# A decoder layer with routed experts on one core: the turn from the router to the first expert rearranged

## Chip, cores, metric
One of the eight cores of one Trainium2 chip runs the whole kernel. Times are device microseconds (us) of one execution; less is better. MiB below is 1,048,576 bytes.

## What is computed
Input: 256 tokens of width 2048 in float32, one condition vector `c`, and the weights of one layer. Cut to what matters here:

```python
mod = silu(c) @ w_ada + b_ada                  # six vectors: sh1, sc1, gt1, sh2, sc2, gt2
h = rmsnorm(x, g1) * (1 + sc1) + sh1
mixed = concat(recurrence(h @ w_in), attention(h @ w_in)) @ w_out
x = x + gt1 * mixed
h = rmsnorm(x, g2) * (1 + sc2) + sh2
group = argmax of 4 group logits; two best of its 8 experts; weights = softmax(two) * p_group
y = sum over the 2 chosen experts e of weight_e * (silu(h @ w_gate[e]) * (h @ w_up[e])) @ w_down[e]
out = rmsnorm(x + gt2 * y, g_final)
```

There are 32 experts of 12 MiB each, and all of them are run, each on at most 64 tokens (slots); a branch at the end covers an overflow.

## The kernel before
The order of the work is written out by hand: each engine runs its instructions strictly in program order, and a tile's first reader waits for its writer. All weights come through one queue, SP's. `load` appends to a list, and `pump` (line 122) issues the head of the list as soon as a 1 MiB slot is free, so loads go in list order and a load waits behind every earlier one. There are 7 slots `w` from the start; 3 `x` and 2 `TT` are added during the output projection and 3 `v` at its end, 15 in all. `drop` gives a slot back after its last reader.

**Projection stage.** The work runs in units of half a MiB of weight. `split(i + 3)` prepares the pieces of a unit three units ahead: ACT rounds the weight to `wh` (line 453), DVE makes the rest `wl` (line 456). PE then runs 24 short or 12 long matmuls on it (lines 462 to 470). First come 20 tiles of `w_in`. Between them go 12 pairs of tiles of `w_ada` for sc1 and sh1 (`pair_load`, after the tiles whose numbers stand in `PAIRS`); each pair is used by an event (`gem`), half of it on PE (line 358) and half on DVE (line 352), and after four pairs `fold1` (line 388) makes a quarter of h from them. Then come 28 more tiles of `w_in` with 64 rows of `w_ada` (1 MiB each, for sc2, sh2, gt1, gt2 in this order) spread between them by `ROWS_B`; a row costs four matmuls (`row`, `product`) or two DVE instructions. Attention and recurrence run beside as jobs, some steps after each unit.

**Output projection.** Two halves (`part` 1, then 0) of four column blocks `n` of four units each. `out_evac` ends a block: in part 0 DVE adds the two halves (957), multiplies by gt1 (958) and adds x into `xp` (960), each for the two halves `m` of the tokens, and ACT squares for the norm (962). Two units later `router_part` transposes `xp` into `h2t` on PE (975), copied out by ACT (979) and DVE (977), and one unit after that `router_logits` (988) adds to the 36 logits. For the last block these stand alone at the end.

**Turn.** `rs2` is the norm's factor (POOL's power, 110). Lines 1125 to 1178 choose: the logits `el`, the first maximum of the group logits, then of the experts, that one masked out, and the first maximum again, with the weights in between; the choice `sel` goes through three matmuls (1173 to 1175) to slot numbers. `one_hots` makes the matrices G and Sg, `gather` (1210) collects the tokens of two experts into XT in four quarters `kq`, `back` prepares the way back.

**Experts.** They run in pairs. `gate_up` takes four pieces per expert, each of one gate and one up tile, and drops both tiles after the piece. Between pieces stand, for the first pair, the spread of gt2 (`gate`, lines 776 and 777), the overflow count and `natural` (the residual copied to `xr` by ACT). Then come the next pair's gather and `down` (eight tiles).

Of the kernel before, what the change touches and what calls it, by code (L numbers as in the profile page):

```python
# [16 lines left out]
P = 128  # L17
# [23 lines left out]
PAIRS = (0, 2, 3, 5, 7, 8, 10, 12, 13, 15, 17, 18)  # L41
AHEAD = 8
ROWS_B = (3, 2, 3, 2, 2, 2, 2) * 4
# [12 lines left out]
def layer_kernel(ctx: ExitStack, tc: tile.TileContext, x, c, w_ada, b_ada, g_norm_mix, w_in, lb_logits,  # L56
# [158 lines left out]
    assert not rows  # L215
# [732 lines left out]

    def out_evac(part, n):
        sl = slice(512 * n, 512 * n + 512)  # L950
        xin = None if part else take(("x", n // 2))[:, :, 512 * (n % 2):512 * (n % 2) + 512]
        for m in range(2):
            if part:
                ACT.activation(tok[8 + n][:, m, :], banks["o"][m], AF.Copy)
                continue
            tmp = right["ex1"].tile([P, 512], F32, name="tmp", tag="tmp", bufs=TB)
            DVE.tensor_tensor(tmp, banks["o"][m], tok[8 + n][:, m, :], op=ALU.add)
            DVE.tensor_tensor(tmp, tmp, vec[GT1][:, sl], op=ALU.mult)
            xs = right["xp"][:, m, 4 * n:4 * n + 4, :]
            DVE.tensor_tensor(xs.rearrange("t r p -> t p r"), xin[:, m].rearrange("t (p r) -> t p r", r=4),  # L960
                              tmp.rearrange("t (p r) -> t p r", r=4), op=ALU.add)
            ACT.activation(tmp, xs.rearrange("t r p -> t (r p)"), AF.Square, accum_out=right["ss4"][:, m, n:n + 1])
        if not part and n % 2:
            free.append((mixa, f"TT{n // 2}"))
            drop(("x", n // 2))

    def router_part(n):

        xp, ht = right["xp"], right["ex1"].tile([P, 4, S], F32, name="h2t", tag="h2t", bufs=1)
        for b in range(2):  # L970
            t = mx()
            tv = t.rearrange("p (a s) -> p a s", a=2)
            for a in range(2):
                for m in range(2):
                    PE.transpose(tv[:, a, m * P:m * P + P], xp[:, m, 4 * n + 2 * b + a, :], ident)
            if b:
                DVE.tensor_copy(ht[:, 2:4, :], tv)
            else:
                ACT.activation(ht[:, 0:2, :], tv, AF.Copy)
        return ht  # L980

    def router_logits(n, ht):
        if not n:
            banks["r"] = hold("lg")[0]
        for r in range(4):
            k = 4 * n + r
            for m in range(2):
# [38 lines left out]
    for i, u in enumerate(units):  # L1026
# [31 lines left out]
        else:  # L1058
            first, last = u["kq"] % 2 == 0 and not u["half"], u["kq"] % 2 and u["half"]
            bk, k0 = "o", (4 * u["kq"] + 2 * u["half"] + 8) % 16  # L1060
            if not u["part"] and not u["n"] and first:
# [3 lines left out]
                open_router()  # L1065
        if first:
# [3 lines left out]
        for r in range(2):  # L1070
# [38 lines left out]

    ht = router_part(3)  # L1110
# [14 lines left out]
    for m in range(2):  # L1125
        DVE.scalar_tensor_tensor(el[:, m], banks["r"][:, 64 * m:64 * m + 36], rs2[:, m:m + 1], cb, op0=ALU.mult, op1=ALU.add)

# [6 lines left out]
    def first_max(vals, n, wts):  # L1134

        v, q, w = rt(), rt(n), rt()
        DVE.tensor_reduce(v, vals, axis=AX.X, op=ALU.max)
        DVE.tensor_tensor(q, vals, bcast(v[:, :, None], [P, 2, n]), op=ALU.is_equal)
        DVE.tensor_tensor(q, q, bcast(wts[:, None, :], [P, 2, n]), op=ALU.mult)
        DVE.tensor_reduce(w, q, axis=AX.X, op=ALU.max)  # L1140
        DVE.tensor_tensor(q, q, bcast(w[:, :, None], [P, 2, n]), op=ALU.is_equal)
        return v, q

    gl, ee = el[:, :, 0:4], el[:, :, 4:36]
    gmx, gsel = first_max(gl, 4, w4)
    gex, pg = rt(4), rt()
    DVE.tensor_tensor(gex, gl, bcast(gmx[:, :, None], [P, 2, 4]), op=ALU.subtract)
    ACT.activation(gex, gex, AF.Exp)
    DVE.tensor_reduce(pg, gex, axis=AX.X, op=ALU.add)
    DVE.reciprocal(pg, pg)  # L1150
    em = rt(NE)
    emv = em.rearrange("p m (g e) -> p m g e", g=4)
# [366 lines left out]
```

## Time and profile before
| | us |
|---|---|
| median of 3 runs | 1568.62 (1567.92 to 1569.22) |
| profiled execution, its own time | 1570.29 |
| its span, first to last instruction | 1568.5 |
| PE busy | 1495.2 (95%) |
| DVE busy | 641.4 (41%) |
| ACT busy | 378.1 (24%) |

The profiled execution lies 1.67 us above the median of the runs. The mean granted clock of TensorE was 0.977 of its full 2.4 GHz; the lower level is 1.2 GHz, shown as 0.50. In a timeline row the first two numbers are the start and the length of a merged group in us, then come the engine, the line, the operation, output<-input and the count, and in brackets how long the engine stood idle before and who released it. PE's busy share is modelled and also covers waits inside a stream of matmuls, so it doesn't say alone that PE is the bound.

### The profile page before, as it was taken

The numbers are of one execution on the slowest core, as the hardware profiler recorded it, in microseconds if no ns is written. First come the engines' busy times: TensorE is split into PE (matmuls) and PEld (weight loads), VectorE is DVE, ScalarE is ACT, GpSimd is POOL, SyncE is SP. The second block draws the span as 40 slices with busy tenths as digits, with TensorE's granted clock in tenths as the row PEclk, the third lists the DMA queues.
The fourth block names the chain that finished last, engine by engine and source line by source line (L and its number), as shares of the span: only waits on it lengthen the run. The fifth ranks groups of instructions, "written<-read, shape, count | busy, mean of one in ns | idle before, by whom it ended". The sixth has DMA issues, their size and how long they took to land. (4 is left out here: it accounts for less than half of the span.)

```text
span 1568.5 us, 21452 instructions
## 1 busy us (share of the span) xinstructions
PE 1495.2 (95%) x8911; PEld 873.5 (56%) x8911; DVE 641.4 (41%) x1193; ACT 378.1 (24%) x666; POOL 12.5 (1%) x23
## 2 busy tenths in 40 slices
PE   5799989999999987999999999999999999999996
PEld 2687877877678765434443553553554544544532
DVE  3566887556465553132332322332322322232224
ACT  3344332452535523211110110110110101101112
POOL 0000000000000000000000000000000000000000
PEclk9889999999999997999999999999999999999998
DMA  9989989979994654999999999999999999999995
GB/s 355 310 293 333 330 343 396 378 308 350 361 380 155 221 184 195 423 420 421 421 421 421 421 421 421 421 421 421 421 421 421 421 421 421 420 421 421 421 410 205
DMA packets 128271, 579.15 MB, mean 369 GB/s; under 512 B 16983, under 2 KB 17063, under 8 KB 71847
## 3 DMA queue, kind: packets, MB, share of 16 engines
q1 hardware_dynamic: 128170, 577.74, 92.2%
q8 instruction: 72, 1.18, 0.3%
q14 instruction: 29, 0.24, 0.0%
HBM read 575.60 MB, written 2.10 MB: 368 GB/s over the span
## 5 line engine op out<-in xcount | busy, mean ns | idle before, releaser
L1300 DVE TENSOR_TENSOR xr<-st,xr 128x512 f32<-128x512 f32 x124 | 84.4, 690 | 364.6 <-PE st L1299 364.6
L1239 PE MATMUL gu<-w,XT 128*64 128x512 f32 x488 | 224.4, 605 | 1.0 <-DMA w<-in_w_expert_up_dram 1.0
L1237 PE MATMUL gu<-w,XT 128*64 128x512 f32 x472 | 218.1, 605 | 0.0
L456 DVE TENSOR_TENSOR wl<-w,wh 128x1024 fp32r<-128x1024 f32 (+1 forms) x126 | 152.8, 1217 | 150.0 <-ACT wh L453 148.4
L453 ACT ACTIVATE wh<-w 128x1024 fp32r<-128x1024 f32 (+1 forms) x126 | 132.1, 1051 | 206.5 <-PE pj L470 97.8
L1263 PE MATMUL dn<-w,he 128*64 128x512 f32 x492 | 162.4, 594 | 0.0
L462 PE MATMUL pj<-hi,wh 128*128 128x256 f32 x480 | 143.2, 298 | 3.4 <-ACT hi L346 3.4
L463 PE MATMUL pj<-lo,wh 128*128 128x256 f32 x480 | 138.8, 289 | 0.1
L464 PE MATMUL pj<-hi,wl 128*128 128x256 f32 x480 | 138.4, 288 | 0.0
L1210 PE MATMUL dn<-G,xp 128*128 128x128 f32 x1024 | 121.1, 278 | 1.2 <-DVE G L1193 1.2
L1210 PEld LDWEIGHTS dn<-G,xp 128*128 128x128 f32 x1024 | 119.4, 194 | 3.4 <-issue 2.1
L1270 DVE SCALAR_TENSOR_TENSOR ye<-dn,ws,gt2b 128x512 f32<-128x512 f32 x64 | 47.7, 745 | 166.3 <-PE dn L1263 166.3
L1237 PEld LDWEIGHTS gu<-w,XT 128*64 128x64 f32 x472 | 61.3, 138 | 81.2 <-issue 79.7
L346 ACT ACTIVATE yh<-ye 128x512 fp32r<-128x512 f32 x64 | 40.3, 630 | 274.0 <-DVE ye L1270 274.0
L358 PE MATMUL ev<-w,crep 128*32 128x512 f32 x616 | 79.6, 629 | 27.5 <-DMA w<-in_w_ada_dram 27.5
L462 PEld LDWEIGHTS pj<-hi,wh 128*128 128x128 f32 x480 | 94.6, 197 | 18.5 <-issue 12.9
L1245 ACT ACTIVATE gub<-gu 128x512 f32<-128x512 f32 x32 | 19.1, 598 | 345.8 <-PE gu L1239 345.8
L1237 PE MATMUL gu<-x,XT 128*64 128x512 f32 x224 | 101.7, 596 | 0.0
L463 PEld LDWEIGHTS pj<-lo,wh 128*128 128x128 f32 x480 | 94.6, 197 | 0.5 <-DVE lo L347 0.4
L1239 PE MATMUL gu<-v,XT 128*64 128x512 f32 x208 | 94.5, 597 | 0.0
L464 PEld LDWEIGHTS pj<-hi,wl 128*128 128x128 f32 x480 | 94.4, 197 | 0.0
L1239 PE MATMUL gu<-x,XT 128*64 128x512 f32 x200 | 90.8, 597 | 0.0
(322 smaller groups left out, 2248.5 us busy)
## 6 DMA issues: line engine op xcount, KB each, us to landing
w<-in_w_ada_dram SPq DMA_DIRECT2D x96, 1024.0 KB, 8.8
w<-in_w_expert_up_dram SPq DMA_DIRECT2D x61, 1024.0 KB, 19.8
w<-in_w_expert_down_dram SPq DMA_DIRECT2D x61, 1024.0 KB, 19.8
w<-in_w_expert_gate_dram SPq DMA_DIRECT2D x59, 1024.0 KB, 19.8
w<-in_w_in_dram SPq DMA_DIRECT2D x48, 1024.0 KB, 8.3
x<-in_w_expert_gate_dram SPq DMA_DIRECT2D x28, 1024.0 KB, 19.8
v<-in_w_expert_up_dram SPq DMA_DIRECT2D x26, 1024.0 KB, 19.8
x<-in_w_expert_up_dram SPq DMA_DIRECT2D x25, 1024.0 KB, 19.8
```

The lines of the kernel that those rows point to most:

```text
L358: PE.matmul(out_[32 * quad:32 * quad + 32], crep[:, k, :], wt, start=first, stop=last, skip_group_check=True, tile_position=(0, 32 * quad))
L453: ACT.activation(wh, src, AF.Copy)
L456: (POOL if subs[i % len(subs)] else DVE).tensor_tensor(wl, src, wh, op=ALU.subtract)
L462: PE.matmul(o, wh[:, c_], hi(k), start=bool(start and j % 2 == 0), stop=False, skip_group_check=True)
L463: PE.matmul(o, wh[:, c_], lo(k), start=False, stop=False, skip_group_check=True)
L464: PE.matmul(o, wl[:, c_], hi(k), start=False, stop=bool(stop), skip_group_check=True)
L1210: PE.matmul(tv[:, r, :], xp[:, m, 4 * kq + r, :], G[:, m, :], start=m == 0, stop=m == 1)
L1237: PE.matmul(t[0:64], xk, wg[:, r, :], start=k == 0, stop=k == KD - 1, skip_group_check=True, tile_position=(0, 0))
L1239: PE.matmul(t[64:128], xk, wu[:, r, :], start=k == 0, stop=k == KD - 1, skip_group_check=True, tile_position=(0, 64))
L1263: PE.matmul(t[64 * j:64 * j + 64], he[j][:, f, :], wd[j], start=f == 0, stop=f == 3, skip_group_check=True, tile_position=(0, 64 * j))
L1270: DVE.scalar_tensor_tensor(ye, t, ws, gt2b[:, 512 * n:512 * n + 512], op0=ALU.mult, op1=ALU.mult)
L1300: DVE.tensor_tensor(xr[:, m, sl], t, xr[:, m, sl], op=ALU.add)
```

## The change
Seven edits, in order of the program. (1) The pairs of `w_ada` move one tile later for eight of the twelve (`PAIRS`). (2) The rows are spread two to a tile, three in the last four tiles; four rows of gt2 are left over and are loaded after the last tile of `w_out`. They are used at the end: two before `router_part(3)`, one after it, one after `router_logits(3)` (`ROWS_Z`, `more_rows`), and gt2's vector is ended there. (3) `out_base` forms x + gt1 * (first half) ahead, in place, so that `out_evac` has a product and a sum left; the squares move behind the transposes. (4) In the output projection and the router the loops run one half of the tokens after the other. (5) The choice uses a masked copy, one MAX8 per token half, MATCH_REPLACE and a comparison; the weights move to `weights`, called in the first expert. (6) Of the first gather only the first quarter is done before the first gate/up piece; each of the next three stands ahead of one of the first three pieces, and `back` behind the fourth. Sg of the first pair is made after the second piece. (7) The spread of gt2, the overflow count and `natural` of the first pair move from the first to the second expert.

```diff
-PAIRS = (0, 2, 3, 5, 7, 8, 10, 12, 13, 15, 17, 18)
+PAIRS = (1, 3, 4, 6, 8, 9, 11, 12, 14, 15, 17, 18)
-ROWS_B = (3, 2, 3, 2, 2, 2, 2) * 4
+ROWS_B = (2,) * 24 + (3,) * 4
+ROWS_Z = (2, 1, 1)
-    assert not rows
+    last_rows = [row_load() for _ in range(len(rows))]
+    def out_base(n):
...
+        for m in range(2):
+            p1 = tok[8 + n][:, m, :]
+            DVE.tensor_tensor(p1, p1, vec[GT1][:, sl], op=ALU.mult)
+            DVE.tensor_tensor(p1, p1, xin[:, m], op=ALU.add)
+        if n % 2:
+            drop(("x", n // 2))
     def out_evac(part, n):
...
-            DVE.tensor_tensor(tmp, banks["o"][m], tok[8 + n][:, m, :], op=ALU.add)
-            DVE.tensor_tensor(tmp, tmp, vec[GT1][:, sl], op=ALU.mult)
+            DVE.tensor_tensor(tmp, banks["o"][m], vec[GT1][:, sl], op=ALU.mult)
...
-            ACT.activation(tmp, xs.rearrange("t r p -> t (r p)"), AF.Square, accum_out=right["ss4"][:, m, n:n + 1])
     def router_part(n):
...
+        for m in range(2):
+            jk = right["ex1"].tile([P, 512], F32, name="jk", tag="tmp", bufs=TB)
+            ACT.activation(jk, xp[:, m, 4 * n:4 * n + 4, :].rearrange("t r p -> t (r p)"), AF.Square,
+                           accum_out=right["ss4"][:, m, n:n + 1])
...
+                soon(i + 1, out_base, 0)
...
+        if bk == "o":
+            for m in range(2):
+                for r in range(2):
+                    three(banks[bk][m], k0 + r, m, wh[:, r], wl[:, r], first and r == 0, last and r == 1)
...
+                if u["n"] < 3:
+                    soon(i + 2, out_base, u["n"] + 1)
                 soon(i + 2, lambda n=u["n"]: soon(ev_at[0] + 2, router_logits, n, router_part(n)))
...
+    more_rows(ROWS_Z[0])
     ht = router_part(3)
+    more_rows(ROWS_Z[1])
     router_logits(3, ht)
+    more_rows(len(last_rows))
+    ended_vec[GT2] = vector_end(GT2)
...
+    for m in range(2):
+        DVE.copy_predicated(em[:, m].rearrange("p (g e) -> p g e", g=4), bcast(gsel[:, m, :, None], [P, 4, 8]),
+                            ee[:, m].rearrange("p (g e) -> p g e", g=4))
+    for m in range(2):
+        DVE.max(m8[:, m], em[:, m])
+    DVE.tensor_copy(top2[:, :, 0:2], m8[:, :, 0:2])
+    for m in range(2):
+        DVE.match_replace(left[:, m], top2[:, m], em[:, m], TAKEN)
+    DVE.tensor_scalar(sel, left, -2e38, None, op0=ALU.is_lt)
...
-    gather(made, range(4))
-    cur = made[2], back(made, 0)
+    gather(made, (0,))
+    first_made, cur = made, (made[2], None)
...
         def after0(kq):
...
-            if not e0:
-                if kq == 0:
-                    gate(GT2, gs2, lambda: bank("st", 2))
-                elif kq == 1:
-                    overflow()
-                natural(kq)
+            if not e0 and kq == 1:
+                weights()
+                slots_of(first_made[1], 0)
...
         def after1(kq):
+            if not e0:
+                natural(kq)
+                if kq == 1:
+                    gate(GT2, gs2, lambda: bank("st", 2))
+                elif kq == 2:
+                    overflow()
...
-        gu = gate_up(e0, 0, XT, after0)
+        gu = gate_up(e0, 0, XT, after0, None if e0 else lambda kq: gather(first_made, (kq,)))
+        if not e0:
+            back_ = back(first_made, 0)
```

`gate_up` calls its new argument `ahead(kq + 1)` before each of its first three pieces.

## Rows read from the trace of the kernel before

**Rows 1.** The page's 40 slices of the span (39.2 us each): PE in tenths, GB/s.
```profile
PE   5799989999999987999999999999999999999996
...
GB/s 355 310 293 333 330 343 396 378 308 350 361 380 155 221 184 195 423 420 421 421 421 421 421 421 421 421 421 421 421 421 421 421 421 421 420 421 421 421 410 205
```

**Rows 2.** Busy time by stretch: PE, PEld, DVE, ACT, POOL; then PEclk, DMA share, GB/s.
```profile
600.00:628.00 28.00, 25.61 (x132) 15.38 (x134) 8.66 (x39) 11.09 (x18) 0.00 (x0) 0.82 0.29 109
616.00:628.00 12.00, 11.32 (x42) 3.49 (x42) 0.14 (x1) 8.08 (x10) 0.00 (x0) 0.86 0.63 228
620.00:624.00 4.00, 4.00 (x14) 1.23 (x12) 0.00 (x0) 4.00 (x5) 0.00 (x0) 0.57 0.74 303
```

**Rows 3.** Timeline, SP's queue: expert weight loads issued.
```profile
616.31 0.33 SPq L135 DMA_DIRECT2D x<-in_w_expert_up_dram  x1
...
646.97 0.39 SPq L135 DMA_DIRECT2D x<-in_w_expert_gate_dram  x1
658.47 0.33 SPq L135 DMA_DIRECT2D w<-in_w_expert_up_dram  x1
```

**Rows 4.** Timeline, PE, the last two matmuls of the output projection.
```profile
583.37 0.40 PE L469 MATMUL pj<-wl,hi 128*128 128x512 f32 x1
583.60 0.40 PE L470 MATMUL pj<-wh,lo 128*128 128x512 f32 x1
```

**Rows 5.** Timeline, DVE, from the last output block to the router's choice.
```profile
583.34 0.69 DVE L957 TENSOR_TENSOR tmp<-pj,TT 128x512 f32<-128x512 f32 x1 [4.20 <-PE pj L470]
...
587.11 1.03 DVE L960 TENSOR_TENSOR xp<-w,tmp 128x512 f32<-128x512 f32 x1
...
593.58 0.42 DVE L1126 SCALAR_TENSOR_TENSOR el<-lg,rs,cb 128x36 f32<-128x36 f32 x2 [2.56 <-PE lg L988]
594.03 0.16 DVE L1137 TENSOR_REDUCE r<-el 128x2 f32<-128x8 f32 x1
594.22 0.17 DVE L1138 TENSOR_TENSOR r<-el,r 128x8 f32<-128x8 f32 x1
```

**Rows 6.** Timeline, PE, router logits, slot matmuls, first gather.
```profile
579.24 1.87 PE L988 MATMUL lg<-wrA,h2t 128*128 128x36 f32 x16
...
589.84 3.63 PE L988 MATMUL lg<-wrA,h2t 128*128 128x36 f32 x16
600.50 0.61 PE L1173 MATMUL mx<-r,jp 128*128 128x32 f32 x2 [7.03 <-DVE r L1168]
...
603.17 8.97 PE L1210 MATMUL dn<-G,xp 128*128 128x128 f32 x64 [1.21 <-DVE G L1193]
```

**Rows 7.** Timeline, PE, waits of the projection stage (start, length, instructions, [idle before]).
```profile
51.95 1.06 PE L358 MATMUL ev<-w,crep 128*32 128x512 f32 x8 [1.23 <-DMA w<-in_w_ada_dram]
...
67.43 1.94 PE L358 MATMUL ev<-w,crep 128*32 128x512 f32 x8 [8.52 <-DMA w<-in_w_ada_dram]
...
88.83 1.44 PE L393 MATMUL mx<-ones,acc 128*128 128x1 f32 x6 [3.27 <-DVE acc L352]
...
223.79 1.06 PE L358 MATMUL ev<-w,crep 128*32 128x512 f32 x8 [1.45 <-DMA w<-in_w_ada_dram]
```

**Rows 8.** Groups by form, DVE, first 500 us: busy us, mean ns | idle before.
```profile
L512 DVE MAX8 m<-sc 128x8 f32<-128x128 f32 x8 | 2.3, 291 | 0.2
...
L513 DVE MATCH_VALUE_LOAD sc<-m,sc 128x8 f32 x16 | 1.5, 92 | 0.6
```

**Rows 9.** Groups by line, PE, 612.6 to 616.2: busy us, mean ns | idle before.
```profile
L1237 PE MATMUL gu<-x,XT 128*64 128x512 f32 x8 | 3.6, 598 | 0.0
```

**Rows 10.** Busy time by stretch, columns as in rows 2.
```profile
92.00:96.00 4.00, 4.00 (x19) 4.00 (x20) 2.44 (x8) 0.99 (x2) 0.00 (x0) 0.50 1.04 386
```

**Rows 11.** Timeline, PE, router transposes of the second output block.
```profile
559.76 0.98 PE L975 MATMUL mx<-ident,xp 128*128 128x128 f32 x7 [1.48 <-DVE xp L960]
```

**Rows 12.** The page's costliest groups: the splits on DVE and ACT.
```profile
L456 DVE TENSOR_TENSOR wl<-w,wh 128x1024 fp32r<-128x1024 f32 (+1 forms) x126 | 152.8, 1217 | 150.0 <-ACT wh L453 148.4
L453 ACT ACTIVATE wh<-w 128x1024 fp32r<-128x1024 f32 (+1 forms) x126 | 132.1, 1051 | 206.5 <-PE pj L470 97.8
```

More of the change, by code (lines that the diff above doesn't have):

```diff
@@ L1165, in layer_kernel @@
[L1165 to L1171 removed]
+    gl, ee = el[:, :, 0:4], el[:, :, 4:36]
+    gmx, gw, gq, top2, m8 = rt(), rt(), rt(4), rt(8), rt(8)
@@ new lines, in layer_kernel @@
+    em, left, sel, comb, slot = rt(NE), rt(NE), rt(NE), rt(NE), rt(NE)
+    gsel = ex1.tile([P, 2, 4], I32, name="gsel")
+    DVE.memset(em, -1e38)
+    DVE.memset(top2, 3e38)
+    for m in range(2):
+        DVE.scalar_tensor_tensor(el[:, m], banks["r"][:, 64 * m:64 * m + 36], rs2[:, m:m + 1], cb, op0=ALU.mult, op1=ALU.add)
+    DVE.tensor_reduce(gmx, gl, axis=AX.X, op=ALU.max)
+    DVE.tensor_tensor(gq, gl, bcast(gmx[:, :, None], [P, 2, 4]), op=ALU.is_equal)
+    DVE.tensor_tensor(gq, gq, bcast(w4[:, None, :], [P, 2, 4]), op=ALU.mult)
@@ new lines, in layer_kernel @@
+    DVE.tensor_reduce(gw, gq, axis=AX.X, op=ALU.max)
+    DVE.tensor_tensor(gsel, gq, bcast(gw[:, :, None], [P, 2, 4]), op=ALU.is_equal)
+    for m in range(2):
+        DVE.copy_predicated(em[:, m].rearrange("p (g e) -> p g e", g=4), bcast(gsel[:, m, :, None], [P, 4, 8]),
+                            ee[:, m].rearrange("p (g e) -> p g e", g=4))
+    for m in range(2):
+        DVE.max(m8[:, m], em[:, m])
+    DVE.tensor_copy(top2[:, :, 0:2], m8[:, :, 0:2])
+    for m in range(2):
+        DVE.match_replace(left[:, m], top2[:, m], em[:, m], TAKEN)
@@ L1178, in layer_kernel, with weights @@
     DVE.tensor_scalar(slot, slot, -1.0, None, op0=ALU.add)
+    def weights():
+        gex, pg, e2 = rt(4), rt(), rt()
+        DVE.tensor_tensor(gex, gl, bcast(gmx[:, :, None], [P, 2, 4]), op=ALU.subtract)
+        DVE.tensor_tensor(comb, em, bcast(m8[:, :, 0:1], [P, 2, NE]), op=ALU.subtract)
+        DVE.tensor_tensor(e2, m8[:, :, 1], m8[:, :, 0], op=ALU.subtract)
+        ACT.activation(gex, gex, AF.Exp)
+        ACT.activation(comb, comb, AF.Exp)
+        ACT.activation(e2, e2, AF.Exp)
+        DVE.tensor_reduce(pg, gex, axis=AX.X, op=ALU.add)
+        DVE.reciprocal(pg, pg)
+        DVE.tensor_scalar(e2, e2, 1.0, None, op0=ALU.add)
+        DVE.reciprocal(e2, e2)
+        DVE.tensor_tensor(e2, e2, pg, op=ALU.mult)
+        DVE.tensor_tensor(comb, comb, sel, op=ALU.mult)
+        DVE.tensor_tensor(comb, comb, bcast(e2[:, :, None], [P, 2, NE]), op=ALU.mult)
     gs2 = ended_vec[GT2]
@@ L1227, in back, with gate_up @@
         return ST, ws
-    def gate_up(e, j, XT, after):
+    def gate_up(e, j, XT, after, ahead=None):
         t = bank("gu", 2)
         for kq in range(4):
+            if ahead and kq < 3:
+                ahead(kq + 1)
             wg, wu = take(("gate", e, kq)), take(("up", e, kq))
```

74 lines of the change are left out of this document (21 added, 53 removed).

## The prediction, made before the changed kernel ran

> **What bounds the kernel now.** I read the slices first [rows 1]. From the seventeenth slice (627 us) almost to the end the weights arrive at a flat 420 to 423 GB/s, which is 2.49 us for a tile of 1 MiB. The experts' stage is a transfer stream, and its end moves by as much as the time at which the stream starts to run without gaps. Before it, in slices 13 to 16, only 155 to 221 GB/s arrive while PE is busy: the output projection waits for PE, and its transfers have time to spare. In the first twelve slices both are high.
>
> So two things can move the end: when the output projection is over, and how much of the stream is lost at the turn. The finer windows price the turn [rows 2]: from 600 to 628 us only 109 GB/s arrived, 2.9 MiB, which the full rate moves in 7.2 us. So 28 - 7.2 = 20.8 us of stream are lost. All 15 slots are full of gate and up tiles by then; the next load is issued at 616.31, when the first piece has given its slots back [rows 3].
>
> **Part 1, the turn up to the first gather.** The chain in the rows is: last matmul of the projection, evacuation, transposes, logits, choice, slots, gather.
>
> *Evacuation.* The last matmul starts at 583.60, matmuls follow at 0.23 us [rows 4]. Before, the first token half is ready three matmuls before the end, DVE begins at 583.34 and the last `xp` ends at 588.14: six instructions of 0.69, 0.69 and 1.03 [rows 5]. After, the first half is ready six matmuls before the end (582.65) and each half takes 0.69 + 1.03; the second starts at 584.4, when both its bank and DVE are ready, and ends at 586.2. Saved: 1.9 us. The removed work isn't gone: `out_base` puts 16 DVE instructions of 0.69 us into part 0, where the evacuation loses eight; net eight more, 5.5 us (part 2).
>
> *Transposes and logits.* PE idled and ran the last logits at half clock, 3.63 us against 1.87 for the same 16 records at full clock [rows 6]. After, PE fills the wait with two rows (eight matmuls took 1.06 us when they ran at full clock [rows 7]), transposes the halves by 586.9, runs a row and finishes the logits near 589.5. The norm's factor (two squares on ACT, now behind a copy, then DVE and POOL) I put level with them, so `el` starts at 589.7 instead of 593.58 [rows 5]. Saved: 3.9 us in all.
>
> *Choice.* Before, 593.58 to 600.50, 6.9 us [rows 5, 6]. After, `el` 0.45, five small group instructions at 0.2 from start to start [rows 5], then nine more plus two value loads. MAX8 and MATCH_REPLACE on 32 columns are not in the trace. Bounds: 0.17 as for 8 columns [rows 5] and 0.29 as MAX8 took on 128 columns [rows 8]; I take 0.2, since 32 is nearer to 8. With value loads at 0.09 that makes 0.45 + 1.0 + 1.9 = 3.4 us (3.1 to 4.2). Saved: 3.5 us. The row of 8 columns lasts 0.17 although there is hardly anything to do, so splitting by token halves costs a whole instruction each time, six of them here, 1.2 us; that is inside the 3.4.
>
> The slot matmuls, two DVE instructions and G stay. The weights and Sg leave the chain; ACT and DVE do them while PE is in the second and third pieces, and if that cover were short, `back` would wait, at most their 3 to 4 us. First gather: 603.17 - 7.4 = 595.8 us.
>
> **Part 1, from the first gather to the stream.** The first piece's slots come back after two gather quarters (5.4 us, the first at half clock, out of the 8.97 of all four [rows 6]) and one piece (3.6 us busy [rows 9], some 3.5 until the next could start): 604.7 instead of 616.2. That looks like 11.5 us, but the work up to `down` is only reordered. Eight pieces, the gather, `back`, the spread of gt2 with its wait and the next gather stand between the first gather and the first `down` slot at 658.47 [rows 3], on PE in a row. Is that path or the transfer the bound there? Sixteen loads were issued from 616.31 to 646.97 [rows 3]. By 628 us 228 GB/s x 12 us = 2.6 MiB had arrived [rows 2], from then on one per 2.49 us, so at 658.47 14.8 had, and 1.2 MiB or 2.9 us of cover were left, less the start of a new transfer. The stream barely lived through that stretch. So the PE path sets the restart: its 7.4 us are passed on, plus about 1 us of that cover.
>
> The transfers would allow more. The four rows take four of the 15 slots and one slot is freed earlier, so 8 MiB instead of 5 are left to load after the projection: 20.8 - 3 x 2.49 = 13.3 us. The Trainium skill, page DMA: Bandwidth & Descriptors, section Specifications, gives about 358 GB/s as a core's limit for HBM; by it, an estimate, a tile would take 2.93 us and this end would be 28 - 8.5 - 3 x 2.93 = 10.7 us. The trace differs, with 420 to 423 GB/s over twenty slices [rows 1], and the measurement decides. **Taken: 8.4 us**; ends 6 (the choice at its bound, 1 us of new waits) and 13.3. The moved spread, count and `natural` do not shorten the path; the same 4 matmuls wait for the same ACT copies, in the second expert. The rows' four loads pass through SP's queue ahead of the gate tiles, during the output projection, where the queue waits for slots and not for transfers; behind them are only gate tiles, and those that now come last are needed by the second expert. POOL's only step, the power, stands where it stood.
>
> **Part 2, up to the end of the output projection.** *Pairs.* Small loads (norm and bias vectors, router weights) stand in SP's queue ahead of the third pair: PE stands 8.52 us until 67.43, after five units [rows 7]. A unit takes 12 x 0.23 = 2.8 us [rows 4]. With the pairs later, the gems stand at units 0, 4, 6, 10 instead of 0, 2, 4, 8, so PE has two more units (5.6 us) to run before it needs the third pair, which lands one load later (1 MiB at 386 GB/s [rows 10] is 2.7 us). Saved: 2.9 us. The next wait, 3.27 us at `fold1` [rows 7], comes from DVE, late with `masks`; with the gem two units later the masks are done before it: about 1.5 us left, 1.8 saved. After it PE ran at half clock, 0.50 in 92 to 96 [rows 10], in all about 9 us that cost 4.5; half of this, 2.3 us, should go. What could take it back is the transfers, 293 to 396 GB/s in the first seven slices [rows 1]. I take 6 of these 7; ends 0 and 9.
>
> *Rows.* Four rows fewer on PE, 4 x 0.53 = 2.1 us. Two waits for rows like that at 223.79 [rows 7], 2.9 us, come from three rows to a tile; I take 1.5 of them. If the transfers bind instead of PE there, four tiles fewer are 10 us.
>
> *Output projection.* In blocks 1 and 2 the transposes wait 1.5 us for `xp` [rows 11]. The shorter evacuation ends these waits. But `out_base` puts 2.8 us of DVE ahead of the copy into `h2t`: after a unit's end come rounding 1.05 and split 1.22 [rows 12], base 2.8 and copy 0.7, 5.8 us; PE has the transposes, one unit and half the logits to run, 1.1 + 2.8 + 0.9 = 4.8, so the logits wait 1 us in three blocks. Sum: -3 + 3, I take 0 (ends -3 and +5).
>
> **Sum.** 1570.3 (the profiled execution, span and 1.8 around it) - 8.4 - 6 - 2.1 - 1.5 = 1552.3. The median of the runs lies 1.7 below that execution, so 1550.6, rounded 1550.5.
>
> **The rivals.** *The front gives nothing.* The projection stage is as much transfer as PE, and what the pairs save is waited for later. For: the early slices move 310 to 396 GB/s, not far from the 420 of the experts. Against: PE shows 9 tenths or more in nearly all slices from the fourth on [rows 1]. Then only the turn counts: 1568.6 - 8.4 = 1560.
>
> *The turn gives all that the transfers allow.* If the pair's PE path has slack that I don't see, 13.3 instead of 8.4: 1545.5. Against it is the cover of 2.9 us; for it, that I estimated that cover from rates.
>
> *DVE binds the output projection.* Four splits, evacuation, copy and base are 4.9 + 3.4 + 0.7 + 2.8 = 11.8 us for a block in which PE needs 11.2 + 1.1 + 1.9 = 14.2; if the in-order queue makes the pieces late all the same, the added 5.5 us are lost: 1556.
>
> *The clock stays at half through the first experts: slower.* Place: 595 to 640 us. Before, nearly 9 us of uninterrupted gather went ahead of the first piece, and the clock was back at 1.00 by then; a later wait, at the spread of gt2, was followed by 0.57 in 620 to 624 [rows 2]. After, quarters and pieces alternate, with a wait for DVE or ACT possible at each.  A piece at 1.2 GHz, the lower of the clock's two levels, takes 3.5 us more; six of the eight (21 us) eat the whole gain, all eight give 1550.5 + 28 = 1578.5. Against: the waits that I find are under 1 us, and PE has other work between. The Trainium skill, page TensorE: Matmul & The Clock Gate, section "A second HAM failure mode: psum-queue depth-cycling", tells of short idles between groups of matmuls that make the clock swing between its levels; by that rule the interleaving would be a loss. The trace has one case like it, the 0.57 above.
>
> *The change doesn't do what it says:* the rows could stay late and the queue stand behind them, so that only the choice is shorter: 1568.6 - 3.5 = 1565.
>
> **Chances.** Forecast 0.60, front nothing 0.14, full turn 0.10, DVE 0.07, clock 0.06, not as said 0.03. The range holds 0.8 of this: its low end is the full turn with 4 us more from the front, 1541; its high end the front without gain and 1 us less at the turn, 1561; the clock case and the extremes are left out. A difference below 0.2%, 3.1 us, can't be told from none. Slower: 0.06, of which the clock case is most; same 0.04, from the cases near the bound; faster 0.90.
>
> **What would show it.** The gap at the third pair near 7 us and the `fold1` gap near 1.5; the output projection's last matmul at about 574 instead of 584 us; from it to `el` 6 us (before 10), `el` to the slot matmuls 3.4, first gather 12 after the last matmul (19.6 before); the first slot back 9 us after that; the stream without a gap up to the wait for the first `down` slot, and there a gap of 1 to 4 us. I am wrong if the last matmul comes at 584 (front), if the stream has no gap at `down` (full turn), or if the granted clock is 0.50 in the pieces.

## The result and the profile after

The changed kernel takes 1551.8 us in the median of five runs (1551.65 to 1554.41); the kernel before took 1568.62 (1567.92 to 1571.04) beside it. The ratio is 0.9894, with a 95% interval of 0.9880 to 0.9909. Forecast were 1550.5 us and a range of 1541 to 1561: **faster, as forecast, and 1.3 us off**. The profiled run is itself the one of 1551.8 us, with a span of 1550.0, 18.5 less than before.

The page of the changed kernel, its slices (38.75 us each), PE and GB/s, to set beside [rows 1]:

```profile
PE   5899999999999999999999999999999999999996
...
GB/s 355 308 334 329 338 359 387 329 277 358 349 390 149 270 205 418 342 422 419 422 421 421 421 420 422 421 421 421 421 421 420 422 421 422 420 421 421 421 410 200
```

The flat stream begins a slice earlier, but the seventeenth slice, 342, has a hole in it. A table of the places at which the prediction can be held against the traces (us from the start of the span):

| | before | forecast | after |
|---|---|---|---|
| projection's last matmul ends | 584.0 | 574 | 571.3 |
| from there to `el` | 9.6 | 6 | 5.9 |
| `el` to the slot matmuls | 6.9 | 3.4 | 3.0 |
| projection's end to the first gather | 19.2 | 12 | 11.6 |
| first gather to the first slot given back | 13.1 | 9 | 9.2 |
| first gather to the first `down` slot | 55.3 | 54.3 | 58.1 |
| first `down` slot to the end | 910.0 | | 909.0 |

So the sum came from three terms: 12.7 us ahead of the turn (forecast 9.6), 7.6 in the turn up to the first gather (7.4), 1.0 at the end, less 2.8 lost between gather and `down` (about 1 gained was forecast). A miss of 3.1 us one way and one of 3.8 us the other nearly cancelled, so it is partly luck that the whole lies only 1.3 us off. The rows that show it, the timeline of PE after (start, length, engine, line, operation, output<-input, count, [idle before]):

```profile
69.98 1.93 PE L359 MATMUL ev<-w,crep 128*32 128x512 f32 x8 [5.75 <-DMA w<-in_w_ada_dram]
...
90.05 1.05 PE L394 MATMUL mx<-ones,acc 128*128 128x1 f32 x8 [1.27 <-DVE acc L353]
...
570.88 0.40 PE L471 MATMUL pj<-wh,lo 128*128 128x512 f32 x1
571.21 1.06 PE L359 MATMUL ev<-x,crep 128*32 128x512 f32 x8
572.09 1.04 PE L359 MATMUL ev<-w,crep 128*32 128x512 f32 x8
573.06 1.15 PE L982 MATMUL mx<-ident,xp 128*128 128x128 f32 x8
574.13 1.07 PE L359 MATMUL ev<-w,crep 128*32 128x512 f32 x8
575.13 1.98 PE L1000 MATMUL lg<-wrA,h2t 128*128 128x36 f32 x16
577.04 1.06 PE L359 MATMUL ev<-w,crep 128*32 128x512 f32 x8
580.22 0.61 PE L1184 MATMUL mx<-r,jp 128*128 128x32 f32 x2 [2.11 <-DVE r L1182]
...
582.89 5.60 PE L1243 MATMUL dn<-G,xp 128*128 128x128 f32 x32 [1.21 <-DVE G L1222]
```

The two waits of the front are at the forecast sizes: 8.52 has become 5.75 (about 7 was said) and 3.27 has become 1.27 [rows 7]. From 571.21 on PE is hardly ever idle: it runs two rows, transposes, a row, logits (1.98 us, not the 3.63 at half clock of [rows 6]), a row; only the choice leaves a hole, 2.11 us instead of 7.03. The four `ev` groups are the four rows left over, a row each, 1.06 us.

The timeline of DVE after, the choice, to set beside [rows 5]:

```profile
577.21 0.42 DVE L1166 SCALAR_TENSOR_TENSOR el<-lg,rs,cb 128x36 f32<-128x36 f32 x2 [1.11 <-PE lg L1000]
...
578.66 0.30 DVE L1175 COPY_PREDICATED r<-gsel,el 128x32 f32<-128x32 int32 x2
578.89 0.29 DVE L1178 MAX8 r<-r 128x8 f32<-128x32 f32 x2
...
579.50 0.18 DVE L1181 MATCH_REPLACE8 r<-r,r 128x32 f32<-128x32 f32 x1
579.59 0.08 DVE L1181 MATCH_VALUE_LOAD r<-r,r 128x8 f32 x1
```

`el` waits for the logits, not for the norm's factor. A replacement on 32 columns costs 0.18, and two MAX8 0.29 together: the value taken in the prediction, 0.2, was a little high.

Then comes what the prediction missed. PE and SP after, around the spread of gt2, now in the second expert (two timelines), and the stretches around it (busy PE, PEld, DVE, ACT, POOL; PEclk, DMA share, GB/s):

```profile
615.03 1.13 PE L777 MATMUL st<-gs,first 1*128 1x512 f32 x4
616.84 2.56 PE L777 MATMUL st<-gs,first 1*128 1x512 f32 x4 [0.68 <-ACT gt2b L778]
619.33 1.11 PE L1272 MATMUL gu<-w,XT 128*64 128x512 f32 x1
```

```profile
615.54 0.38 SPq L136 DMA_DIRECT2D x<-in_w_expert_gate_dram  x1
625.40 0.33 SPq L136 DMA_DIRECT2D w<-in_w_expert_up_dram  x1
...
629.52 0.38 SPq L136 DMA_DIRECT2D w<-in_w_expert_gate_dram  x1
641.02 0.33 SPq L136 DMA_DIRECT2D w<-in_w_expert_up_dram  x1
```

```profile
592.00:612.00 20.00, 20.00 (x112) 9.43 (x112) 4.07 (x22) 6.31 (x13) 0.00 (x0) 1.00 1.01 414
618.00:624.00 6.00, 6.00 (x15) 1.48 (x14) 0.00 (x0) 3.16 (x4) 0.00 (x0) 0.50 1.02 429
626.00:630.00 4.00, 4.00 (x24) 1.76 (x21) 0.00 (x0) 0.85 (x2) 0.00 (x0) 1.00 0.82 297
638.00:642.00 4.00, 4.00 (x20) 1.29 (x18) 0.11 (x1) 0.40 (x2) 0.00 (x0) 1.00 0.08 16
```

The four spread matmuls (two records each) wait for ACT's copies and hold PE for 4.3 us, and the pieces behind them run at a granted clock of 0.50, one matmul 1.06 us instead of 0.59. For 9.9 us no slot is given back (615.54 to 625.40), and the stream breaks off twice: 297 GB/s in 626 to 630, 16 in 638 to 642. In all some 7.4 us of stream are lost between 622 and 646 (an estimate: 292 GB/s over these 24 us, against 422); the prediction had expected one gap of 1 to 4 us.

The way from the first gather to the first `down` slot as one window, before and after:

```profile
603.20:658.50 55.30, 54.62 (x304) 29.72 (x306) 10.79 (x42) 19.22 (x33) 0.00 (x0) 0.94 0.69 283
```

```profile
582.90:641.00 58.10, 57.42 (x304) 30.20 (x306) 12.10 (x52) 21.15 (x37) 0.00 (x0) 0.91 0.91 377
```

PE has the same 304 matmul records in both and is idle for 0.7 us in both. The lower clock costs 3.3 us before (0.06 of 55.3) and 5.2 after (0.09 of 58.1): that is about 1.9 of the 2.8 us lost. How long the clock stays low behind the spread isn't settled by the place alone. Of the six kernels here that have the whole spread in the second expert, four lose about 3.4 us there, like this one, and two about 1.7, like the kernel before (the runs with the rows back and with the first gather whole).

### The profile page after: what moved, and what is told of

It is laid out like the page before. It is cut to its first block, busy times and chain, and to the rows that moved or that the text cites. A ratio compares the mean times of both kernels' runs of the same rounds, so it can differ in the third digit from the quotient of the medians.

```text
span 1550.0 us, 21497 instructions
## 1 busy us (share of the span) xinstructions
PE 1495.4 (96%) x8927; PEld 871.1 (56%) x8927; DVE 639.1 (41%) x1193; ACT 378.3 (24%) x667; POOL 12.5 (1%) x23
## 5 line engine op out<-in xcount | busy, mean ns | idle before, releaser
L1274 PE MATMUL gu<-w,XT 128*64 128x512 f32 x504 | 230.8, 602 | 0.6 <-DMA w<-in_w_expert_up_dram 0.6
L1272 PE MATMUL gu<-w,XT 128*64 128x512 f32 x488 | 225.3, 606 | 0.0
L1298 PE MATMUL dn<-w,he 128*64 128x512 f32 x428 | 135.8, 593 | 0.0
L1272 PEld LDWEIGHTS gu<-w,XT 128*64 128x64 f32 x488 | 63.9, 138 | 87.0 <-issue 85.2
L1272 PE MATMUL gu<-x,XT 128*64 128x512 f32 x208 | 94.7, 597 | 0.0
L1274 PEld LDWEIGHTS gu<-w,XT 128*64 128x64 f32 x504 | 65.5, 138 | 48.6 <-issue 31.0
```

The source lines that it names most:

```text
L1272: PE.matmul(t[0:64], xk, wg[:, r, :], start=k == 0, stop=k == KD - 1, skip_group_check=True, tile_position=(0, 0))
L1274: PE.matmul(t[64:128], xk, wu[:, r, :], start=k == 0, stop=k == KD - 1, skip_group_check=True, tile_position=(0, 64))
L1298: PE.matmul(t[64 * j:64 * j + 64], he[j][:, f, :], wd[j], start=f == 0, stop=f == 3, skip_group_check=True, tile_position=(0, 64 * j))
```

## The experiments

Each run of an experiment was timed beside the kernel before; medians of before were 1569.5, 1570.75 and 1571.35 us in the three groups, so a ratio says more than a difference of medians between groups; such differences below can be off by 1 to 3 us for that reason. All edits but one are to the changed kernel.

**The pairs alone put back.**

```diff
-PAIRS = (1, 3, 4, 6, 8, 9, 11, 12, 14, 15, 17, 18)
+PAIRS = (0, 2, 3, 5, 7, 8, 10, 12, 13, 15, 17, 18)
```

> The changed kernel with the old places of the w_ada pairs and nothing else undone. Theory (the later pairs are worth what the trace shows as the lead after the first forty units, 7.2 us): the last matmul of the output projection comes 6 to 8 us later than in the changed kernel and the whole takes 1557.5 to 1560 us; the waits for the third pair (8.5 us) and at the fold (3.3 us) are back. Rival (the projection stage is bound by transfers, and the lead would have come anyway from the rows): 1551 to 1553 us.

Measured: 1559.74 us (1558.72 to 1560.21), ratio 0.9938 (0.9922 to 0.9955). By the medians the pairs are worth 7.9 us (by the ratios 6.9), 6 were forecast. PE's timeline of this run:

```profile
67.00 1.94 PE L359 MATMUL ev<-w,crep 128*32 128x512 f32 x8 [8.27 <-DMA w<-in_w_ada_dram]
...
89.41 1.81 PE L394 MATMUL mx<-ones,acc 128*128 128x1 f32 x8 [3.27 <-DVE acc L353]
```

Both waits are back at their old sizes. Against the changed kernel that is 2.5 and 2.0 us. In two places the lower clock costs another 1.7 us each: behind the second wait it is 0.76 in 86 to 100 us (0.88 after), and it is 0.72 in 138 to 150 (0.86 in the changed kernel's 134 to 146). That makes 7.9. But only the waits are surely the pairs': with the pairs in their new places the clock in 86 to 100 us is 0.76 too in the two runs with three edits (below), and the stretch near 140 us costs 3.4 us in one of them and nothing in the other.

**The rows alone put back** (no row left for the turn):

```diff
-ROWS_B = (2,) * 24 + (3,) * 4
+ROWS_B = (3, 2, 3, 2, 2, 2, 2) * 4
...
-    ended_vec[GT2] = vector_end(GT2)
+    if GT2 in held:
+        ended_vec[GT2] = vector_end(GT2)
```

> The changed kernel with all 64 rows of w_ada back in the projection stage in the old pattern; no row is left for the turn. Theory (a row costs PE eight records of 0.13 us, about 1.0 us, not 0.53, and two waits for rows of 1.45 us come back): the output projection ends 4 to 7 us later than in the changed kernel; at the turn PE idles longer before the choice, but the choice does not wait for PE, so the whole takes 1555.5 to 1559 us. Rival of the prediction's price (0.53 us a row and half of the waits): 1554 to 1555.5 us. Rival (transfers bind there): 10 us, 1561 us and more.

Measured: 1560.92 us, widely spread (1555.01 to 1563.43), ratio 0.9934 (0.9910 to 0.9958): 9.1 us by the medians (6.3 by the ratios), more than the theory's, near the 10 of the case in which the transfers bind; but the trace shows 2.7 us of waits for rows, not 10. The profiled run is the longest of the four. PE's timeline there, and a window of this run and the same of the changed kernel:

```profile
219.26 1.06 PE L359 MATMUL ev<-w,crep 128*32 128x512 f32 x8 [1.26 <-DMA w<-in_w_ada_dram]
...
221.74 1.94 PE L359 MATMUL ev<-w,crep 128*32 128x512 f32 x8 [1.41 <-DMA w<-in_w_ada_dram]
```

```profile
220.00:228.00 8.00, 6.59 (x36) 4.38 (x33) 6.62 (x10) 0.66 (x2) 0.00 (x0) 0.57 1.03 411
```

```profile
220.00:228.00 8.00, 7.49 (x66) 5.77 (x64) 5.89 (x15) 3.97 (x6) 0.00 (x0) 1.00 1.03 407
```

The two waits (2.7 us) are whole again, not half, and this time the clock falls behind them: 0.57 over 8 us is 3.4 us lost. In the kernel before the same two waits (1.45 and 1.44 us, at 223.79 and 226.29) were followed by the full clock:

```profile
220.00:228.00 8.00, 5.11 (x45) 3.04 (x43) 8.00 (x9) 2.08 (x2) 0.00 (x0) 1.00 1.03 411
```

So these 3.4 us can't be put down to the waits alone. Two rows more on PE are 2.1. The span is 11.6 us above that of the changed kernel, and the last 3.4 of it are two longer stretches of half clock near 100 and 145 us (0.84 over 22 us and 0.79 over 16, against 0.92 and 0.89). Such stretches come and go between runs with the same front, and the four times of this kernel, 8.4 us apart, may come from that: the mean granted clock is 0.975 in the two longest runs (1563.43 and 1563.2) and 0.980 in the others (1558.64 and 1555.01). The other three have no trace.

Whether the two parts need each other is not shown. The projection ends at 579.2 with the pairs back, at 583.7 with the rows back, at 571.3 with both new and 584.0 with both old: by these traces the rows alone gain 4.8 us, the pairs alone 0.3, both 12.7. But the 0.3 rests on the longest of four runs, and with one 8.4 us shorter the two would simply add. A comparison without that run: in the traces of before and after, the first row on PE behind the last pair starts at 202.22 and 195.06, a lead of 7.2 us (forecast 6), and 5.6 more come up to 537 us (forecast 3.6).

**The first gather whole**, ahead of the first piece (the interleaving undone):

```diff
-    gather(made, (0,))
+    gather(made, range(4))
...
-        gu = gate_up(e0, 0, XT, after0, None if e0 else lambda kq: gather(first_made, (kq,)))
+        gu = gate_up(e0, 0, XT, after0)
```

> The changed kernel with the first gather done whole ahead of the first gate/up piece; the way back stays behind the fourth piece. Theory (the PE path from the first gather to the first down slot is only reordered by the interleaving, and that path sets when the stream starts again): within 1.5 us of the changed kernel, 1550.5 to 1553.5 us, although the first slot comes back 3.5 us later (12.5 us after the first gather instead of 9.2). Rival (the early return of the first slots is what keeps the stream going): 3 us or more, 1555 us and up.

Measured: 1550.06 us (1549.8 to 1550.89), ratio 0.9879 (0.9862 to 0.9895), 0.4 us below the theory's bounds. SP's timeline of this run, the first slot given back and the first `down` slot (the gather starts at 582.63):

```profile
595.49 0.33 SPq L136 DMA_DIRECT2D w<-in_w_expert_up_dram  x1
...
638.46 0.33 SPq L136 DMA_DIRECT2D w<-in_w_expert_up_dram  x1
```

The slot comes back later (12.9 us behind the gather instead of 9.2) and the first `down` slot sooner: 55.8 us behind the gather instead of 58.1. About 1.7 of these 2.3 us are a shorter stretch of half clock behind the spread (0.55 in 617 to 620 and 0.88 in 620 to 623, where the changed kernel has 0.56, 0.50 and then 0.80 in 623 to 626). The interleaving gains nothing; the earlier slot is not what the end hangs on.

**The spread of gt2 early**, two pieces behind the last row, two behind the slot matmuls, all ahead of the gather:

```diff
     ended_vec[GT2] = vector_end(GT2)
+    gate(GT2, ended_vec[GT2], mx, (0, 1))
...
+    gate(GT2, ended_vec[GT2], mx, (2, 3))
...
-                if kq == 1:
-                    gate(GT2, gs2, lambda: bank("st", 2))
-                elif kq == 2:
+                if kq == 2:
```

> The changed kernel with the spread of gt2 (four short matmuls and four copies) taken out of the second expert's pieces and put into PE's idle time at the router: two of the four behind the last row, two behind the slot matmuls. Theory (the PE path of the first pair sets the restart at the first down slot, and there the spread costs 4.4 us of PE and about 3 us more because the granted clock falls to 0.50 behind it): the way from the first gather to the first down slot shrinks from 58.1 us to 51 to 54 us and the whole takes 1544.5 to 1548 us; it can't gain more than the 7.4 us of stream that the changed kernel still loses between 622 and 646 us. Rival (the stream is the bound there already): 1551 to 1553 us.

Measured: 1547.72 us (1546.64 to 1549.99), ratio 0.9864 (0.9847 to 0.9880). PE's timeline:

```profile
581.49 2.08 PE L777 MATMUL mx<-gs,first 1*128 1x512 f32 x4
584.73 6.71 PE L1246 MATMUL dn<-G,xp 128*128 128x128 f32 x32 [1.17 <-ACT gt2b L778]
```

The gather starts 1.8 us later, since the second half stands in its way; the `down` slot still comes 3.9 us sooner (637.1), 52.4 us behind the gather. Time and way lie inside the theory's bounds.

**The spread split**: the first half as above, the second in the second expert, where two banks then do for two pieces. The edit also puts ACT's copies of `natural` behind the spread.

```diff
+    gate(GT2, ended_vec[GT2], mx, (0, 1))
...
-                natural(kq)
                 if kq == 1:
-                    gate(GT2, gs2, lambda: bank("st", 2))
+                    gate(GT2, gs2, lambda: bank("st", 2), (2, 3))
                 elif kq == 2:
                     overflow()
+                natural(kq)
```

> The changed kernel with the spread of gt2 taken apart: its first two pieces of 512 through the matmul banks straight behind the last row, its other two behind the first gather, through two banks, so that no piece waits for a copy. My theory: the changed kernel's way from the first gather to the first down slot (58.1 us) is longer than before's (55.3) because the spread stalls TensorE for 4.4 us and TensorE works at the lower clock behind it. With the spread apart there is no such stall and at most one half-clock stretch of 3.4 us behind the turn; the first gather starts no later than in the changed kernel (582.9, against 584.7 in the run with the whole spread ahead of the gather); the first down slot comes by 637 to 639 and the time is 1545.5 to 1547.5 us. The rival: the way to the first down slot is set by the stream of the weights, which the spread does not hold up; then the first down slot stays at 640 to 641 and the time at 1551 to 1553.

Measured: 1548.6 us (1546.94 to 1550.38), ratio 0.9865 (0.9848 to 0.9882); the profiled run is the 1546.94. Windows of this run:

```profile
582.80:635.40 52.60, 52.60 (x300) 28.96 (x302) 12.06 (x52) 19.98 (x35) 0.00 (x0) 0.96 1.00 416
...
618.00:624.00 6.00, 6.00 (x33) 2.06 (x29) 0.15 (x1) 3.73 (x5) 0.00 (x0) 1.00 1.01 416
```

The gather starts where it did (582.8) and the `down` slot comes 5.6 us sooner, with PE busy without a gap and 1.00 instead of 0.50 behind the spread. That is the theory, in the trace; the median lies 1.1 us above its bounds, for the other three runs took 1.6 to 3.4 us longer. They have no trace; their mean granted clock is 0.981 to 0.982, against 0.983 here.

**The logits queued ahead of the next base** in the output projection:

```diff
             if not u["part"]:
+                soon(i + 2, lambda n=u["n"]: soon(ev_at[0] + 2, router_logits, n, router_part(n)))
                 if u["n"] < 3:
                     soon(i + 2, out_base, u["n"] + 1)
-                soon(i + 2, lambda n=u["n"]: soon(ev_at[0] + 2, router_logits, n, router_part(n)))
```

> The changed kernel with the logits' matmuls of a chunk queued ahead of the base of the next chunk in the output projection. My theory: the logits matmuls wait 2.3 us in two waits for VectorE's h2t because VectorE has the next chunk's base before it; in the other order the waits go and TensorE ends the projection up to 2.3 us sooner, 1549.3 to 1550.8 us in all. The rival: VectorE is full there, and the base that now comes later holds up the next chunk's evacuation for as long; the time stays at 1551 to 1552.5, or rises if the delay of the base is longer.

Measured: 1546.83 us (1545.72 to 1548.95), ratio 0.9854 (0.9837 to 0.9872), 2.5 us below the theory's bounds. In the waits of the changed kernel (total, times, longest) stood

```profile
PE lg L1000 <- DVE h2t L985: 2.3, 2, 1.2
```

and no such row is left. The projection ends 5.9 us sooner, more than the 2.3. Up to 524 us the lead is 1.5: one stretch of half clock near 180 us is absent (0.79 in 178 to 186 after, 1.00 here), in code that is the same. The other 4.4 arise in the output projection: 2.3 of waits and the clock behind the second of them. The same window of the changed kernel and of this run:

```profile
552.00:556.00 4.00, 4.00 (x15) 3.32 (x15) 0.75 (x1) 0.00 (x0) 0.00 (x0) 0.57 0.81 270
```

```profile
552.00:556.00 4.00, 4.00 (x19) 3.23 (x18) 3.41 (x4) 1.58 (x2) 0.00 (x0) 1.00 0.42 176
```

0.43 of 4 us is 1.7; a wait of 1.1 us costs more than itself when the clock falls behind it. This stretch stands behind the second wait in all seven traces with the old order and in none of the three with the new one. The first wait, 1.2 us, is followed by such a stretch in only two of the seven (the runs with the rows back and with the spread early).

**One row ahead of the transposes, three behind the logits:**

```diff
-ROWS_Z = (2, 1, 1)
+ROWS_Z = (1, 0, 3)
```

> The changed kernel with one row of the last vector ahead of the transposes at the turn, none behind the transposes and three behind the logits, in place of two, one and one. My theory: TensorE takes about 1.06 us for a row, and a row ahead of the logits delays the logits and all that hangs on them; with one ahead in place of three the way from the end of the projection to the logits takes 4.8 to 5 us instead of 5.8, and the time is 1550.2 to 1551.3 us. The rival: the rows only fill gaps in which TensorE waits for the transposed states to be copied; then the logits come when they did and the time is 1551.5 to 1553.

Measured: 1548.26 us (1546.17 to 1551.25), ratio 0.9861 (0.9841 to 0.9881). PE's timeline:

```profile
570.81 1.07 PE L359 MATMUL ev<-x,crep 128*32 128x512 f32 x8
...
573.14 0.63 PE L982 MATMUL mx<-ident,xp 128*128 128x128 f32 x4 [0.68 <-DVE xp L970]
573.61 2.03 PE L1000 MATMUL lg<-wrA,h2t 128*128 128x36 f32 x16
575.56 2.78 PE L359 MATMUL ev<-w,crep 128*32 128x512 f32 x24
578.74 0.38 PE L1184 MATMUL mx<-r,jp 128*128 128x32 f32 x2 [0.39 <-DVE r L1182]
```

The logits end 4.8 us behind the projection, as expected, although PE now waits 0.68 us for `xp`; the three rows run while DVE chooses, and PE's wait there falls from 2.11 to 0.39. More was gained than expected, because the first gather ran at full clock in this run; in 580 to 586 the changed kernel has 0.50, this run 1.00:

```profile
580.00:586.00 6.00, 5.23 (x38) 4.21 (x40) 3.94 (x17) 1.17 (x4) 0.00 (x0) 1.00 1.02 429
```

That part isn't sure to come again: the run with three edits has the same order of rows and 0.66 there (below).

**The new choice alone, in the kernel before:** `copy_predicated`, MAX8 and `match_replace` in place of the two `first_max` of the experts, and the weights behind the first one-hots.

```diff
-    v1, s1 = first_max(em, NE, w32)
-    DVE.scalar_tensor_tensor(em, s1, -2e38, em, op0=ALU.mult, op1=ALU.add)
-    v2, s2 = first_max(em, NE, w32)
...
+    for m in range(2):
+        DVE.max(m8[:, m], em[:, m])
...
     made = one_hots(0)
+    weights()
     gather(made, range(4))
```

> The kernel before with the new choice of the experts alone: masking by a predicated copy, the top two by one maximum instruction, and the experts' weights computed behind the first one-hots. My theory: the way from the logits in place to the slot matmuls falls from 6.9 to about 3.1 us, since that is what it takes in the changed kernel, and this passes on to the end of the kernel: 1564.8 to 1566 us. The rival: what comes behind the slots (the weights on VectorE and ScalarE in front of the gather's copies, or the stream of the weights) takes the gain back; 1568 to 1570 us.

Measured: 1564.7 us (1564.15 to 1566.45), ratio 0.9965 (0.9952 to 0.9979), 6 us below the kernel before beside it. `el` on DVE and the first slot matmul on PE:

```profile
591.08 0.42 DVE L1138 SCALAR_TENSOR_TENSOR el<-lg,rs,cb 128x36 f32<-128x36 f32 x2 [2.47 <-PE lg L988]
```

```profile
594.08 0.60 PE L1156 MATMUL mx<-r,jp 128*128 128x32 f32 x2 [3.11 <-DVE r L1154]
```

From `el` to the slot matmuls it takes 3.0 us instead of 6.9, and the first `down` slot comes 6.0 us sooner than in the trace of before. 2.5 of these are there ahead of the turn, where nothing is changed (a stretch of half clock at 142 us is absent); 3.9 are the choice, and from the gather to the `down` slot it takes 55.8 us, 0.5 more than before's 55.3. So the choice passes on but for 0.5 us; that the time comes so near the theory's bounds (0.1 us below) is owed in part to the 2.5 us.

**The three edits together**, the spread now in two halves behind the first two pieces of the second expert; and the same **with the first gather whole**.

```diff
-ROWS_Z = (2, 1, 1)
+ROWS_Z = (1, 0, 3)
...
-                natural(kq)
-                if kq == 1:
-                    gate(GT2, gs2, lambda: bank("st", 2))
+                if kq < 2:
+                    gate(GT2, gs2, lambda: bank("st", 2), (2 * kq, 2 * kq + 1))
                 elif kq == 2:
                     overflow()
+                natural(kq)
```

> The changed kernel with three edits together: the logits' matmuls queued ahead of the next chunk's base, the rows of the last vector at the turn one, none and three, and the spread of gt2 in two halves of two pieces behind the first two gate/up pieces of the second expert, through two banks, so that no piece waits for a copy. My theory: the three gains lie at different places of the one chain and add up. From the traces of the single runs: the projection ends 4.3 us sooner (a further 1.4 us in that run came from a stretch of half clock at 187 us, and may or may not come again), the first gather follows the end of the projection 1.7 us sooner (9.9 us in place of 11.6), and the way from the first gather to the first down slot falls from 58.1 to 53 us; in all 11 us less of span, 1539 to 1542 us. The rival: the stream of the weights sets the first down slot once TensorE no longer does; then the way from the gather grows by what the first two give, and the time stays at 1544 to 1547.

> The same three edits, with the first gather whole ahead of the first gate/up pieces instead of piece by piece between them. My theory: the interleaving itself is worth nothing or a little, since it only reorders TensorE's work up to the first down matmul, and the run with the whole gather alone was faster only because its stretch of half clock behind the spread was shorter; without the spread's stall the two agree within 1.5 us. The rival: piece by piece gives back buffers sooner, the stream starts sooner, and the whole gather is slower by 2 us or more; or the interleaving costs TensorE something by itself, and the whole gather is faster by 2 us.

Measured: 1544.81 us (1541.09 to 1546.22), ratio 0.9829 (0.9807 to 0.9851), and with the gather whole **1541.0 us** (1538.42 to 1541.94), ratio 0.9812 (0.9791 to 0.9832), the best of all kernels here. The first stays 3 us short of the theory, at a time that its rival named: its profiled run lost 2.1 us near 90 to 150 us, in unchanged code. From the projection's end to the gather it takes the 9.9 us of the theory, from the gather to the `down` slot 54.6 instead of 53, for half clock at the first gather. The rival's mechanism isn't what the trace shows: PE is busy for 53.9 of these 54.6 us. A window of this run, and two of the one with the whole gather:

```profile
578.00:583.00 5.00, 4.38 (x25) 4.41 (x26) 1.57 (x7) 0.00 (x0) 0.00 (x0) 0.66 1.01 424
```

```profile
575.00:628.00 53.00, 51.11 (x303) 27.66 (x304) 13.17 (x56) 20.98 (x37) 0.00 (x0) 1.00 1.01 422
628.00:644.00 16.00, 16.00 (x78) 5.38 (x76) 4.34 (x12) 1.26 (x2) 0.00 (x0) 1.00 1.01 410
```

With the whole gather the stream hardly breaks any more between the projection and the end (410 GB/s in the second window, some 0.5 us of it lost); 52.4 us lie between gather and `down` slot. So in that run a still earlier `down` slot has little left to win back. The 3.8 us between the two medians, more than the 1.5 expected, are as much as the two profiled runs differ by in clock: 2.1 in the front and 1.7 at the first gather (0.66 over 5 us, against 1.00), and this stretch begins where the two programs still do the same. The other runs fit that: the two short ones of the first kernel (1541.09 and 1541.84 us, at a mean clock of 0.986 and 0.987) lie with those of the second at 0.986 (1541.0 to 1541.94). At equal clock the two kernels agree, as the theory said; whether the interleaving makes the low clock likelier (0.983 in three of five runs with it, 0.986 or more in all five without) stays open. With the time lost to the low clock taken out (an estimate from windows of 2 us) the way from the gather to the `down` slot is 52.8 and 52.9 us with the interleaving, 52.2 and 52.4 without it: it brings nothing in either pair of runs.

## Why the prediction was right

That the whole came within 1.3 us is partly luck, as the table above shows. The steps, one by one:

*What bounds the kernel.* That the end moves with the start of the unbroken stream holds: from the first `down` slot to the end it takes 908.8 to 910.4 us in before, after and the ten experiments. The Trainium skill, page HBM Reference, section Specifications (TRN2), says that a core that streams alone reaches some 425 GB/s. The 422 of the run with the whole gather and three edits agrees with that, and not with the share of 358 by which the prediction worked out its other estimate.

*Evacuation, transposes, logits, choice: right.* 9.6 us became 5.9 up to `el` (6 forecast) and 6.9 became 3.0 (3.4); the run with the choice alone gave 3.9 us by itself.

*"The work up to `down` is only reordered": the step that failed.* The forecast passed the turn's 7.4 us on, with 1 us of cover on top; 4.8 arrived. The prediction noted the spread's wait and the 0.57 behind it in the kernel before [rows 2] and took them to be the same after the move. They were not: half clock filled 618 to 624, where [rows 2] had it in part of 620 to 624, and the way to the first `down` slot, which PE sets, took 58.1 us for the work that took 55.3 before. The stream's extra break at 626 to 630 came of it, but didn't set the end: from the first `down` slot on it takes no longer than before. The run with the spread split gives 5.6 us back, with both the wait and the low clock gone; which of the two is worth how much was not run apart.

*The slower rival* had the right mechanism with the wrong place and size: the clock did go to half, for some 7 us around the first gather and 6 us behind the spread, not for six or eight pieces. So the sign that the prediction named, 0.50 in the pieces, came true for about one piece. Between quarters and pieces it was 1.00 (592 to 612). The Trainium skill, page TensorE: Matmul & The Clock Gate, section "A second HAM failure mode: psum-queue depth-cycling", tells of frequent short idles between groups of matmuls that make the clock swing between its levels. The trace has single idles of that kind: at the spread (0.68 us) the clock was 0.50 over 6 us behind it, at the second of the logits' waits (1.1 us) 0.57 over 4, but behind the first of these waits (1.2 us) it stayed at 1.00, and so it did at the interleaving, for which the rule was named.

*Pairs: right mechanism, sized low.* 7.2 us of lead by the traces of before and after, 7.9 by the medians with the pairs put back, instead of 6; the two waits were worth 2.5 and 2.0 us, near the 2.9 and 1.8 said. The clock was 3.4 instead of 2.3 in that run, but this part comes and goes. Of the sum of 7 the prediction took one off for the transfers, and no new wait for one appears.

*Rows: the term was mis-sized.* A row was priced at 0.53 us, half of the eight records of 1.06; the eight are one row (24 records for three rows in the run with one row first). It came out at the right 2.1 because in the projection stage PE is spared only two of the four (600 records instead of 616); the other two were DVE's, whose share fell from 14 half rows to 10. Of the row waits 1.5 of 2.9 us were taken and all went. This, the pairs and stretches of half clock are the 3 us by which the front was undersold.

*Output projection: right at zero.* The lead was 12.8 us at 537 us and 12.7 at its end. The waits for `h2t` were 2.3 us in two blocks, forecast 3 in three; what they cost in all, 4.4, the other order showed.

*Front gives nothing, DVE binds, not as said:* out, by the projection's end at 571.3, though DVE's base did hold up the logits. *Full turn* (1545.5): not in this kernel; the two runs that only take the spread's stall away reach 1547.7 and 1548.6.

## What to carry to other kernels

A wait of TensorE can cost more than itself: here one of 1.1 us was followed in seven traces of seven by half clock that cost another 1.7, while like waits elsewhere (1.2 us in the same stage, 2.9 us in the kernel before) mostly were not. So look at the granted clock behind each wait and don't take it as given. Moving a step with an internal wait (matmuls paced by another engine's copies through too few banks) is no mere reordering: split it so that its pieces find free banks, and place them where PE has work behind. Work that fills a hole belongs into the hole, behind the producer of the chain and not ahead of it.

## What was not expected of the hardware

The same code, in the same place of the program, runs with or without a stretch of half clock: the front of the changed kernel differs by up to 3.4 us at the row near 195 us between runs of kernels that do not differ there (1.3 sooner to 2.1 later than in the changed kernel). That alone spreads the medians of near variants by a few us, so the traces and the granted clock of each run, more than the medians, tell which edit did what. And `MATCH_REPLACE8` on 32 columns took 0.18 us, hardly more than the 0.17 of an instruction on 8 columns [rows 5].
